# The gates of a two-layer token mixer computed between the steps of its branches and kept in DRAM until the merges

## The chip, the cores and the metric

The kernel runs on one core of a Trainium2 chip, as a single launch. The metric is the device time of that launch in microseconds (us). Before the change the median of three runs is 2623.72 us (2621.29 to 2623.99).

## The reference, cut to what matters

The network has two layers over 512 tokens of width 1024 (256 context tokens and 256 latent tokens). Each layer has a token mixer and a channel mixer, everything in float32. Only the token mixer is touched:

```python
def token_mixer(p, grid_rows, hy_p, cf_p, s5_p, s5_out_p, w_o, init, want_final):
    y_hy = hyena_branch(p[..., :CF_OFF], *hy_p)
    y_cf = conformer_branch(p[..., CF_OFF:S5_OFF], grid_rows, *cf_p)
    y_s5, finals = s5_branch(p[..., S5_OFF:GATE_OFF], s5_p, *s5_out_p, init, want_final)
    g_hy, g_cf, g_s5 = jnp.split(jax.nn.sigmoid(p[..., GATE_OFF:]), N_BRANCH, axis=-1)
    return (g_hy * y_hy + g_cf * y_cf + g_s5 * y_s5) @ w_o, finals
```

Here `p` is one projection of the modulated input, 6144 columns wide: 1536 for the long convolution (hyena), 1024 for the conformer branch (a gated unit and a depthwise convolution of 31 taps), 512 for the state-space branch (S5), and 3 x 1024 for the gates. A gate depends on the mixer's input alone. The second layer's mixer needs only the latent tokens, so it works on 256 of the 512; only the state-space branch there reads all of them.

## The kernel before, in words

**Products.** A float32 product is made of three matmuls: each operand is split into a high and a low part, and `mm3` (L128 to L133) adds high x high, low x high and high x low. A weight chunk of 512 KB (`wchunk`, L135 on) is loaded into a buffer `land`; of each half ScalarE writes the high part `wh` (L123) and VectorE the low part `wl` (L124). There are 4 `land` and 3 `wh`/`wl` buffers, and loads of chunks get a higher priority than what stands around them.

**One gate.** A gate is a tile of 128 channels by the layer's tokens. `gate` computes it from one chunk: `in_tile` issues 24 matmuls (8 slices of the contraction x 3) into a PSUM tile `p`, and ScalarE takes a tanh of it into a tile `mth`. A gate so costs one load, 2 casts on ScalarE, 2 subtractions on VectorE, 24 matmuls and one tanh. A layer has 24 gates, 8 for each branch.

**The mixer.** `mixer` issues, in this order: the projection for S5; the tiles of the long convolution (`hy_in`, short convolutions on VectorE); `s5_main`, four blocks, each of which runs through two groups of small matmuls (`ep`, `yp`) with a chain of VectorE and ScalarE work between them (L399 to L416); `hy_first` and `hy_second`, the two orders of the long convolution, as matmuls with DFT tables (`zc`, `zs` forward, `iv` inverse; in layer 0 for two sequences, in layer 1 for one); `conf_in`, whose result is `ub`; `s5_glu` (`gl`); and three merges, in the order S5, hyena, conformer. Before the last merge stands `conf_conv`, the 31 taps on VectorE (`dc`, L669). Last comes `proj_res`, the output projection (`acc`).

**A merge.** For each of four pairs of output tiles it computes two gates, loads one chunk of the branch's output weights, issues 2 x 12 matmuls (`bo`) and gates the result on VectorE: `mm = (mth + 1) * bo` in the first merge (L858), `mth = (mth + 1) * bo; mm += mth` in the others (L860, L861).

**Modulation work in layer 0.** During the merges of layer 0 a list `bg` of generators is advanced three steps per pair: the modulation vectors for the rest of the layer, whose weights `mw` are multiplied on VectorE (`ma`, L785 and L787; one of them on TensorE, `md`).

**What sets the order.** The program is written in the order above. A scheduler then orders each engine's instructions by priority (program order, chunks earlier) on a modelled timeline, so that matmuls of different steps interleave. On the chip each engine takes its instructions strictly in that order; all DMAs are issued by SyncE (SP), in one order too, and an SP instruction that waits for a buffer or for data holds up the loads behind it.

Of the kernel before, what the change touches and what calls it, by code (L numbers as in the profile page):

```python
# [10 lines left out]
FT = mybir.dt.float32  # L11
# [79 lines left out]
class Net:  # L91
# [264 lines left out]
    def s5_main(self, l, full):  # L356
        nc, sm = self.nc, self.sm
# [10 lines left out]
        f = lambda a: a.rearrange("p g j -> p (g j)")  # L368
        for b in range(NB):
            gs = slice(b * GB, (b + 1) * GB)  # L370
            U = U2[b // 2][:, (b % 2) * GB:(b % 2 + 1) * GB]
            we, wc = [], []
            for r in range(2):
                we.append(self.t4([128, GB, 128], "we", "XL"))
                nc.sync.dma_start(we[r].rearrange("p g m -> p (g m)"), sc["we"][b, r])
            tb = self.t4([128, 2, GB, 64], "tb", "XL")
            nc.sync.dma_start(tb.rearrange("p r g j -> p (r g j)"), sc["tb"][b])
            cs, sn = tb[:, 0], tb[:, 1]
            E = [128, GB, 64]
            ec = self.t4([128, 2, GB, 64], "ec", "XC")  # L380
            for r in range(2):
                ep = self.ps("ep", "aux")
                for g in range(GB):
                    nc.tensor.matmul(ep[:, g * 64:(g + 1) * 64], we[r][:, g], U[:, g], start=True, stop=True)
                nc.scalar.copy(ec[0:64, r].rearrange("p g j -> p (g j)"), ep[0:64])
                nc.scalar.copy(ec[64:128, r].rearrange("p g (s j) -> p g s j", s=2),
                               ep[64:128].rearrange("p (g s j) -> p g s j", g=GB, s=2)[:, :, :, ::-1])
            for r in range(2):
                wc.append(self.t4([128, GB, 128], "wc", "XL"))
                nc.sync.dma_start(wc[r].rearrange("p g m -> p (g m)"), sc["wc"][b, r])  # L390
            mt = self.t4([128, GB, 128], "mt", "U")
            nc.sync.dma_start(mt.rearrange("p g m -> p (g m)"), sc["m"][b])
            md = self.mx.tile(E, FT, name="md", tag="md5", bufs=1)
            nc.scalar.copy(md, mg[:, gs, None].to_broadcast(E))
            nc.gpsimd.memset(md[:, :, 0:1], 0.0)
            rr = self.t4([128, 2, GB, 64], "rr", "XC")
            for r in range(2):
                t1 = self.u2(E, "t1")
                nc.vector.tensor_tensor(rr[:, r], ec[:, r], cs, op=OP.mult)  # L399
                nc.vector.tensor_tensor(t1, ec[:, 1 - r], sn, op=OP.mult)  # L400
                nc.vector.tensor_tensor(rr[:, r], rr[:, r], t1, op=OP.add if r == 0 else OP.subtract)
            z = rr
            for r in range(2):
                nc.vector.tensor_tensor_scan(f(z[:, r]), f(md), f(rr[:, r]), 0.0, op0=OP.mult, op1=OP.add)
            sp = self.t4([128, 2, GB, 64], "sp", "XC")
            q = lambda a: a.rearrange("p g (s j) -> p g s j", s=2)
            for r in range(2):
                t1 = self.u2(E, "t1")
                t2 = self.u2(E, "t2")
                for t in (t1, t2):  # L410
                    nc.gpsimd.memset(t[:, :, 0:1], 0.0)
                nc.vector.tensor_tensor(t1[:, :, 1:], z[:, r, :, :63], cs[:, :, :63], op=OP.mult)
                nc.vector.tensor_tensor(t2[:, :, 1:], z[:, 1 - r, :, :63], sn[:, :, :63], op=OP.mult)
                nc.vector.tensor_tensor(t1, t1, t2, op=OP.subtract if r == 0 else OP.add)
                nc.scalar.copy(sp[0:64, r], t1[0:64])
                nc.scalar.copy(q(sp[64:128, r])[:, :, :, ::-1], q(t1[64:128]))  # L416
            yp = self.ps("yp", "aux")
            for g in range(GB):
                o = yp[:, g * nj:(g + 1) * nj]
                nc.tensor.matmul(o, mt[:, g], U[:, g, j0:], start=True, stop=False)  # L420
                nc.tensor.matmul(o, wc[0][:, g], sp[:, 0, g, j0:], start=False, stop=False)
                nc.tensor.matmul(o, wc[1][:, g], sp[:, 1, g, j0:], start=False, stop=True)
            a = self.u2([128, 512], "ya")
            w = self.u2([128, 512], "yq")
            e = slice(0, GB * nj)
            nc.scalar.activation(w[:, e], yp[:, e], AF.Square)
            nc.vector.scalar_tensor_tensor(w[:, e], w[:, e], 1.0 / 0.044715, yp[:, e], op0=OP.add, op1=OP.mult)
            nc.scalar.activation(w[:, e], w[:, e], AF.Tanh, scale=math.sqrt(2.0 / math.pi) * 0.044715)
            nc.vector.scalar_tensor_tensor(a[:, e], w[:, e], 1.0, yp[:, e], op0=OP.add, op1=OP.mult)
            v = lambda t: t[:, e].rearrange("p (g j) -> p g j", g=GB)  # L430
            for t in range(8):
                nc.sync.dma_start(sc["y"][gs, :, t, j0:].rearrange("g c j -> c g j"), v(a)[t * 16:(t + 1) * 16])

    def s5_glu(self, l, t0):
        nc, sm = self.nc, self.sm
# [172 lines left out]
        return k  # L608

    def hy_first(self, l, v, x0, seqs):  # L610
        k = self.hy_kk(l, 0)
        z1 = {}
        for s in seqs:
            vT = [self.t4([128, 2, 512], f"vT{a}", "Z", FR) for a in range(2)]
            self.hy_turn(v, s, vT)
            x0T = self.t4([128, 2, 512], "x0T", "Z")
            self.hy_turn(x0, s, [x0T])
            z1[s] = [self.t4([128, 2, 512], f"z1{a}", "Z", FR) for a in range(2)]

            def sink(tt, o, s=s, x0T=x0T):  # L620
                t = self.t2([128, 512], "zt")
                self.nc.vector.tensor_mul(t, o, x0T[:, tt])
                self.split(z1[s][0][:, tt], z1[s][1][:, tt], t)
            self.hy_conv(k, vT, 0, sink)
        return z1

    def hy_second(self, l, z1, x1, seqs):

        k = self.hy_kk(l, 1)
        for s in seqs:  # L630
            def sink(c, o, s=s):
                ss = slice(s * 256, (s + 1) * 256)
                self.nc.vector.tensor_mul(x1[c][:, ss], o, x1[c][:, ss])
            self.hy_conv(k, z1[s], 1, sink)
        return x1


# [193 lines left out]
    def gate(self, l, t0, j):  # L831
# [3 lines left out]
        nc.scalar.activation(th[:, t0:], self.in_tile(l, 24 + j, t0)[:, t0:], AF.Tanh, scale=0.5)  # L835
        return th

    def merge(self, l, t0, first, br, src, scale, mm):

        nc = self.nc  # L840
        bH = self.quad("bH", "K", FR)
        bL = self.quad("bL", "XC", FR)
        for j in range(4):
            self.split(bH[j][:, t0:], bL[j][:, t0:], src[j][:, t0:], scale=scale)
        for kp in range(4):
            if first:
                mm.append(self.t4([128, 2, 512], "mm", "Y"))
            ths = []
            for jj in range(2):
                ths.append(self.gate(l, t0, br * 8 + 2 * kp + jj))  # L850
            w = self.wchunk(self.i["w_bo"][l, br, kp], 8)
            for jj, th in enumerate(ths):
                o = self.ps("bo")
                for k in range(4):
                    self.mm3(o[:, t0:], w[jj * 4 + k], (bH[k][:, t0:], bL[k][:, t0:]), k == 0, k == 3)
                d = mm[kp][:, jj, t0:]
                if first:
                    nc.vector.scalar_tensor_tensor(d, th[:, t0:], 1.0, o[:, t0:], op0=OP.add, op1=OP.mult)  # L858
                else:
                    nc.vector.scalar_tensor_tensor(th[:, t0:], th[:, t0:], 1.0, o[:, t0:], op0=OP.add, op1=OP.mult)  # L860
                    nc.vector.tensor_add(d, d, th[:, t0:])  # L861
            self.pump(self.rate)
# [504 lines left out]
    def mixer(self, l, xin):  # L1367

        nc = self.nc
        full = l == 0  # L1370
        nts = (0, 1, 2, 3) if full else (2, 3)
        ws = (0, 1) if full else (1,)
        t0 = 0 if full else 256
        self.hsw = self.sm.tile([128, 12, 4], FT, name="hsw", tag="hsw", bufs=1)
        nc.sync.dma_start(self.hsw, self.i["hysw"][l])
        self.s5_in(l)
        self.pump(1000)
        v = self.hy_in(l, t0, 2)
        x0 = self.hy_in(l, t0, 0)
        self.s5_main(l, full)  # L1380
# [1 line left out]
        x1 = self.hy_in(l, t0, 1)  # L1382
        ho = self.hy_second(l, z1, x1, ws)
        cf = self.conf_in(l, t0)
        mm = []
        so = self.s5_glu(l, t0)
        self.rate = 0
# [14 lines left out]
    def body(self, dbg=None):  # L1402
        nc, tc = self.nc, self.tc
# [15 lines left out]
        c = self.const  # L1419
        self.mo, self.bg, self.rate = {}, [], 0  # L1420
        self.parts = 0
        self.s5sc = [self.s5_scratch(l) for l in range(2)]
        self.kd = [self.dram.tile([2, 2, 128, 2, 512], FT, name=f"kd{l}") for l in range(2)]
        xs = self.dram.tile([128, 4, 1024], FT, name="xs")
# [148 lines left out]
```

## Time and profile before

| | |
|---|---|
| median of three runs | 2623.72 us |
| the profiled execution, its own time | 2638.14 us |
| its span in the trace | 2636.3 us |
| TensorE (PE) busy | 2435.7 us, 92% |
| VectorE (DVE) busy | 2162.4 us, 82% |
| ScalarE (ACT) busy | 1373.0 us, 52% |
| mean granted TensorE clock | 0.941 |

The mixer of layer 0 runs from about 80 to 700 us, that of layer 1 from about 1222 to 1545 us. From 1560 us on the experts of layer 1 run, to the end.

Two marks cut each mixer where the change acts. The *branch stretch* runs from where the last tile of the long convolution's projections is through to the first `ub` (181 to 361.5 us in layer 0, 1276 to 1370.5 us in layer 1): S5 blocks and long convolutions. The *merge stretch* runs from the first `ub` to the first `acc` (361.5 to about 664 us, and 1370.5 to 1522 us): the conformer branch, `gl` and the three merges. A busy share is read against such a stretch, not against the whole span. The start-to-start distance of two matmuls is the time that one takes in a queue of them; the duration that a row gives for one is longer, since they overlap.

### The profile page before, as it was taken

The page shows a single profiled execution, that of the slowest core. Times are in us where ns is not written, and L with a number is a line of the kernel's source. Part 1 is how long each engine was busy: PE and PEld are TensorE (multiplying, and loading weights), DVE is VectorE, ACT ScalarE, POOL GpSimd, SP SyncE. Part 2 cuts the span into 40 slices and gives each one's busy share as a digit, 9 for nine tenths or more (in the row PEclk, how much of TensorE's full clock was granted, in tenths as well). Part 3 has the DMA queues.
Part 4 walks back from the last instruction along what each step waited for, and adds up shares of the span by engine and source line. Part 5 has one row for each costly group of instructions (what it writes and reads, how often), then busy time and mean ns, then how long its engine had stood idle before and what let it go on. Part 6 is the DMA issues. An engine that isn't in the chain of part 4 may idle for free. (4 is left out here: it accounts for less than half of the span.)

```text
span 2636.3 us, 34684 instructions
## 1 busy us (share of the span) xinstructions
PE 2435.7 (92%) x12312; PEld 2029.3 (77%) x12312; DVE 2162.4 (82%) x3182; ACT 1373.0 (52%) x1951; POOL 191.5 (7%) x202
## 2 busy tenths in 40 slices
PE   7888999999899998996999969999999999999986
PEld 2765886788787777885898958888887788878775
DVE  7886789994758988756789778888988789888997
ACT  3343442323453232323444527777877677777864
POOL 1620010000100022211000010000000000000000
PEclk8998899999999999997889979999999999999998
DMA  7455425542325554553545529998999898999984
GB/s 261 156 193 132 160 81 176 176 159 90 108 93 169 184 176 156 197 200 134 188 139 155 179 73 374 354 350 341 351 344 347 329 338 340 351 351 357 359 321 201
DMA packets 147349, 602.52 MB, mean 229 GB/s; under 512 B 41878, under 2 KB 42584, under 8 KB 104160
## 3 DMA queue, kind: packets, MB, share of 16 engines
q1 hardware_dynamic: 147168, 600.24, 63.9%
q8 instruction: 98, 1.61, 0.2%
q14 instruction: 83, 0.68, 0.1%
HBM read 563.96 MB, written 36.21 MB: 228 GB/s over the span
## 5 line engine op out<-in xcount | busy, mean ns | idle before, releaser
L124 DVE TENSOR_TENSOR mwl<-mland,mwh 128x1024 fp32r<-128x1024 f32 x672 | 788.6, 1220 | 79.1 <-ACT mwh L123 65.6
L123 ACT CAST mwh<-mland 128x1024 fp32r<-128x1024 f32 x672 | 675.2, 1052 | 122.6 <-PE mp L133 37.0
L123 ACT CAST wh<-land 128x512 fp32r<-128x512 f32 x396 | 244.6, 621 | 527.7 <-PE p L132 241.4
L124 DVE TENSOR_TENSOR wl<-land,wh 128x512 fp32r<-128x512 f32 x396 | 285.3, 723 | 119.4 <-ACT wh L123 109.2
L131 PE MATMUL p<-hh,wh 128*128 128x256 f32 (+1 forms) x800 | 277.9, 348 | 14.2 <-DVE q L549 8.9
L133 PE MATMUL p<-hh,wl 128*128 128x256 f32 (+1 forms) x800 | 278.2, 350 | 7.0 <-DVE wl L124 6.5
L132 PE MATMUL p<-hl,wh 128*128 128x256 f32 (+1 forms) x800 | 275.5, 345 | 0.1
L1154 PE MATMUL mp<-mwl,xg 128*128 128x512 f32 x560 | 223.9, 402 | 5.2 <-DVE mwl L124 5.1
L1154 PE MATMUL mp<-mwh,xg 128*128 128x512 f32 x560 | 221.2, 397 | 3.5 <-ACT mwh L123 2.8
L787 DVE SCALAR_TENSOR_TENSOR ma<-mw,sv,ma 128x512 f32<-128x512 f32 x196 | 153.5, 806 | 37.1 <-DMA mw<-in_w_mod 36.8
L131 PEld LDWEIGHTS p<-hh,wh 128*128 128x128 f32 x800 | 157.1, 197 | 34.2 <-issue 9.2
L131 PE MATMUL mp<-mwh,xg 128*128 128x512 f32 x448 | 178.0, 397 | 2.6 <-ACT mwh L123 2.6
L132 PE MATMUL mp<-mwl,xg 128*128 128x512 f32 x448 | 177.7, 397 | 1.7 <-DVE mwl L124 1.6
L133 PEld LDWEIGHTS p<-hh,wl 128*128 128x128 f32 x800 | 156.7, 196 | 28.8 <-DVE wl L124 12.0
L133 PE MATMUL mp<-mwh,xg 128*128 128x512 f32 x448 | 176.4, 394 | 0.0
L132 PEld LDWEIGHTS p<-hl,wh 128*128 128x128 f32 x800 | 157.1, 196 | 15.9 <-DVE hl L751 0.3
L133 PE MATMUL fo<-hh,wl 128*128 128x512 f32 (+1 forms) x384 | 147.4, 385 | 1.7 <-DVE wl L124 1.7
L131 PE MATMUL fo<-hh,wh 128*128 128x512 f32 (+1 forms) x384 | 147.6, 385 | 1.3 <-ACT hh L747 0.5
L132 PE MATMUL fo<-hl,wh 128*128 128x512 f32 (+1 forms) x384 | 146.1, 381 | 0.1
L669 DVE SCALAR_TENSOR_TENSOR dc<-ub,cfp,dc 128x512 f32<-128x512 f32 (+1 forms) x240 | 142.9, 622 | 0.6
L1154 PEld LDWEIGHTS mp<-mwl,xg 128*128 128x128 f32 x560 | 106.5, 190 | 30.9 <-DVE mwl L124 10.3
L1154 PEld LDWEIGHTS mp<-mwh,xg 128*128 128x128 f32 x560 | 106.5, 190 | 24.7 <-ACT mwh L123 4.6
(460 smaller groups left out, 4926.9 us busy)
## 6 DMA issues: line engine op xcount, KB each, us to landing
mland<-in_moe_w SPq DMA_DIRECT2D x336, 1024.0 KB, 6.9
mw<-in_w_mod SPq DMA_DIRECT2D x96, 512.0 KB, 3.5
land<-in_w_in SPq DMA_DIRECT2D x96, 512.0 KB, 3.6
land<-in_ffn_w SPq DMA_DIRECT2D x66, 512.0 KB, 4.0
land<-in_w_bo SPq DMA_DIRECT2D x24, 512.0 KB, 3.5
s5we<-weT SPq DMA_DIRECT2D x16, 512.0 KB, 4.0
s5wc<-sw SPq DMA_DIRECT2D x16, 512.0 KB, 2.9
we<-s5we SPq DMA_DIRECT2D x16, 512.0 KB, 5.7
```

The source lines that it names most:

```text
L123: nc.scalar.copy(h, src)
L124: nc.vector.tensor_sub(lo, src, h.bitcast(FT))
L131: nc.tensor.matmul(o, a[0], b[0], start=start, stop=False)
L132: nc.tensor.matmul(o, a[0], b[1], start=False, stop=False)
L133: nc.tensor.matmul(o, a[1], b[0], start=False, stop=stop)
L669: nc.vector.scalar_tensor_tensor(d, ub[:, :R, i:i + 64], cfp[:, j, i:i + 1], d, op0=OP.mult, op1=OP.add)
L787: nc.vector.scalar_tensor_tensor(ac[:, t], wk, self.sv[:, k, t:t + 1], ac[:, t], op0=OP.mult, op1=OP.add)
L1154: self.nc.tensor.matmul(o, x[0][:, i], w[r], start=start and r == 0, stop=stop and r == 1)
```

## The change

A generator `gates` makes the 24 gates of a layer in the order in which the merges use them and writes each to a DRAM tile (`gd`, 256 KB, of which layer 1 uses half). `fill(n)` advances it by n gates. It is called in `s5_main` after each of four blocks (2 gates), in `hy_first` and `hy_second` after each sequence (in layer 0: 1 and 2 gates for each of two sequences; in layer 1: 3 and 3 for its one), which are 14 gates in each layer, and once after `conf_in` for the remaining 10. `merge` no longer computes gates; it loads each from DRAM into an `mth` tile. The kind and number of matmuls, casts and vector instructions stay as they are; 48 writes and 48 loads of gates are added. In `mixer` the call `self.pump(1000)` (which empties `bg`) becomes a loop that pumps and fills while `bg` is not empty.

```diff
@@ s5_main, at the end of each of the four blocks
                 nc.sync.dma_start(sc["y"][gs, :, t, j0:].rearrange("g c j -> c g j"), v(a)[t * 16:(t + 1) * 16])
+            self.fill(2)
@@ hy_first, hy_second, at the end of each sequence
+        full = l == 0
...
             self.hy_conv(k, vT, 0, sink)
+            self.fill(1 if full else 3)
...
             self.hy_conv(k, z1[s], 1, sink)
+            self.fill(2 if full else 3)
@@ new
+    def gates(self, l, t0):
+
+        for br in (2, 0, 1):
+            for j in range(8 * br, 8 * br + 8):
+                th = self.gate(l, t0, j)
+                self.nc.sync.dma_start(self.gd[l][j][:, t0:], th[:, t0:])
+                yield
+
+    def fill(self, n):
+
+        for _ in range(n):
+            next(self.gq, None)
@@ merge
             for jj in range(2):
-                ths.append(self.gate(l, t0, br * 8 + 2 * kp + jj))
+                ths.append(self.t2([128, 512], "mth"))
+                nc.sync.dma_start(ths[-1][:, t0:], self.gd[l][br * 8 + 2 * kp + jj][:, t0:])
@@ mixer
+        self.gq = self.gates(l, t0)
         self.s5_in(l)
-        self.pump(1000)
+        while self.bg:
+            self.pump(4)
+            self.fill(1)
...
         cf = self.conf_in(l, t0)
+        self.fill(24)
@@ body
+        self.gd = [[self.dram.tile([128, 512], FT, name=f"gd{l}_{j}") for j in range(24)] for l in range(2)]
```

The scheduler places the gates further forward than they are written. The first place is on TensorE in layer 0, behind the last projection tile of the long convolution. Before, the transposes (`tq`) of the first convolution follow that tile (`p_1598`) at once:

```order
L133 MATMUL p_1598<-hh_99,wl_1606 128x512
L559 MATMUL tq_2090<-ident_110,q2_1328 128x128 [waits DVE_49,Activation_49]
L559 MATMUL tq_2090<-ident_110,q2_1328 128x128
L559 MATMUL tq_2090<-ident_110,q2_1329 128x128 x2
L493 MATMUL hp_976<-hid_963,w12_951 64x256 [waits DMAHW1_49,PE_49,Activation_49]
L559 MATMUL tq_2097<-ident_110,q2_1328 128x128 [waits DVE_49,PE_49]
```

Now the same place holds gates; these rows are the end of the second (`p_1850`) and the start of the third (`p_1995`), between matmuls of the long convolution's filters (`h3`):

```order
L131 MATMUL p_1850<-hh_147,wh_1857 128x512
L132 MATMUL p_1850<-hl_148,wh_1857 128x512
L133 MATMUL p_1850<-hh_147,wl_1858 128x512
L515 MATMUL h3_1044<-w3_1034,hid_1011 128x512 [waits Activation_49]
L515 MATMUL h3_1049<-w3_1034,hid_1011 128x512 [waits DVE_49]
L131 MATMUL p_1995<-hh_147,wh_1998 128x512 [waits Activation_49]
L132 MATMUL p_1995<-hl_148,wh_1998 128x512
```

Eight gates of layer 0 stand ahead of the first `tq`, six more among the convolutions and S5 blocks behind it. All `yp` and `iv` of the branches now stand ahead of the conformer's projection tiles, where the last of them used to interleave with these.

The second place is SP in the S5 blocks of layer 0, where loads of the blocks' tables (`wc`, `mt`, `we`, `tb`), of filters (`kk`) and of weights (`land`) are issued. Before:

```order
L432 DMA s5y0_87<-ya_1749 16x8x64 x8
L141 DMA land_2886<-in_w_in 128x1024
L390 DMA wc_1899<-s5wc0_82 128x1024
L390 DMA wc_1901<-s5wc0_82 128x1024
L375 DMA we_1977<-s5we0_81 128x1024
```

Now, between a block's result and the next block's table:

```order
L432 DMA s5y0_135<-ya_1797 16x8x64 x8
L848 DMA gd0_1_82<-mth_2728 128x512
L390 DMA wc_2099<-s5wc0_130 128x1024
L390 DMA wc_2101<-s5wc0_130 128x1024
L141 DMA land_3234<-in_w_in 128x1024
L141 DMA land_3272<-in_w_in 128x1024
```

The write of a gate (`gd0_1`) waits for that gate's tanh, and the `wc` loads stand behind it.

The third place is VectorE in the merge stretch of layer 0. Before, the S5 branch's last product (`so`) follows the start of the fourth convolution tile directly:

```order
L654 SCALAR_TENSOR_TENSOR ub<-cth,p 128x8x64
L124 TENSOR_TENSOR wl<-land,wh 128x512
L669 SCALAR_TENSOR_TENSOR dc<-ub,cfp,dc 128x512 x3
L124 TENSOR_TENSOR wl<-land,wh 128x512
L667 TENSOR_SCALAR dc<-ub,cfp 128x512
L461 SCALAR_TENSOR_TENSOR so<-gth,g_3042 128x8x64
```

Now the convolution's taps and the weight splits of the ten gates come between the two, 41 rows in all, of which these are the last:

```order
L674 SCALAR_TENSOR_TENSOR dc<-ub,cfp,dc 128x512 x3
L124 TENSOR_TENSOR wl<-land,wh 128x512
L674 SCALAR_TENSOR_TENSOR dc<-ub,cfp,dc 128x512
L462 SCALAR_TENSOR_TENSOR so<-gth,g_4002 128x8x64
L674 SCALAR_TENSOR_TENSOR dc<-ub,cfp,dc 128x512 x2
```

The taps move ahead of `so`, and all of `ma` now stands behind it, among the `bo` of the merges.

## Rows read from the trace of the kernel before

**Rows 1.** The profile page: span, and busy time of each engine.
```profile
span 2636.3 us, 34684 instructions
...
PE 2435.7 (92%) x12312; PEld 2029.3 (77%) x12312; DVE 2162.4 (82%) x3182; ACT 1373.0 (52%) x1951; POOL 191.5 (7%) x202
```
**Rows 2.** Busy time of each engine by stretch (instructions in brackets), with granted clock.
```profile
core 0: us, PE busy (x) PEld busy (x) DVE busy (x) ACT busy (x) POOL busy (x), PEclk, DMA share, GB/s
181.00:361.50 180.50, 157.72 (x769) 129.30 (x768) 126.37 (x205) 69.61 (x116) 3.50 (x21) 0.87 0.45 130
181.00:262.00 81.00, 63.30 (x228) 44.84 (x227) 50.37 (x85) 29.24 (x52) 0.22 (x2) 0.81 0.51 132
361.50:664.00 302.50, 295.00 (x1318) 232.29 (x1318) 253.80 (x407) 98.34 (x163) 13.39 (x11) 0.97 0.43 143
590.00:664.00 74.00, 72.81 (x334) 62.06 (x335) 33.35 (x57) 26.98 (x46) 0.18 (x1) 0.89 0.27 87
1276.00:1370.50 94.50, 88.96 (x547) 84.28 (x546) 77.88 (x130) 43.71 (x77) 3.29 (x19) 0.80 0.47 148
1370.50:1522.00 151.50, 145.97 (x1151) 141.91 (x1150) 131.97 (x290) 75.30 (x150) 2.09 (x3) 0.98 0.51 164
1482.00:1522.00 40.00, 38.69 (x326) 38.53 (x325) 25.95 (x55) 23.34 (x48) 0.70 (x1) 1.00 0.55 181
```
**Rows 3.** VectorE by line and form, 361.5 to 664 us: busy, mean ns, idle before.
```profile
L669 DVE SCALAR_TENSOR_TENSOR dc<-ub,cfp,dc 128x512 f32<-128x512 f32 x120 | 85.9, 743 | 0.2
L124 DVE TENSOR_TENSOR wl<-land,wh 128x512 fp32r<-128x512 f32 x89 | 61.0, 685 | 28.4 <-ACT wh L123 22.0 <-PE p L133 6.3
L787 DVE SCALAR_TENSOR_TENSOR ma<-mw,sv,ma 128x512 f32<-128x512 f32 x84 | 59.3, 741 | 0.0
```
**Rows 4.** VectorE by line and form, 590 to 664 us.
```profile
L124 DVE TENSOR_TENSOR wl<-land,wh 128x512 fp32r<-128x512 f32 x20 | 13.8, 690 | 24.0 <-ACT wh L123 17.7 <-PE p L133 6.3
```
**Rows 5.** TensorE by line and form, 590 to 664 us: the first of a gate's three matmuls.
```profile
L131 PE MATMUL p<-hh,wh 128*128 128x512 f32 x48 | 19.6, 409 | 0.0
```
**Rows 6.** Timeline of TensorE, layer 0: start, duration; nine starts apart in each pair.
```profile
256.48 0.63 PE L131 MATMUL p<-hh,wh 128*128 128x512 f32 x1
...
260.32 0.62 PE L131 MATMUL p<-hh,wh 128*128 128x512 f32 x1
...
261.25 0.39 PE L131 MATMUL p<-hh,wh 128*128 128x512 f32 x1
...
263.29 0.39 PE L131 MATMUL p<-hh,wh 128*128 128x512 f32 x1
```
**Rows 7.** Timeline of TensorE, layer 1: six starts apart.
```profile
1408.51 0.28 PE L131 MATMUL p<-hh,wh 128*128 128x256 f32 x1
...
1409.23 0.28 PE L131 MATMUL p<-hh,wh 128*128 128x256 f32 x1
```
**Rows 8.** Timeline of VectorE: a weight split and the instruction behind it.
```profile
409.80 0.67 DVE L124 TENSOR_TENSOR wl<-land,wh 128x512 fp32r<-128x512 f32 x1
410.40 0.73 DVE L669 SCALAR_TENSOR_TENSOR dc<-ub,cfp,dc 128x512 f32<-128x512 f32 x1
```
**Rows 9.** Timeline, TensorE and ScalarE: the first S5 block of layer 0.
```profile
248.21 2.18 PE L384 MATMUL ep<-U,we 128*128 128x64 f32 x9 [5.00 <-DMA U<-s5u]
...
255.93 0.58 ACT L386 COPY ec<-ep 64x512 f32<-64x512 f32 x1
...
278.95 0.33 PE L421 MATMUL yp<-sp,wc 128*128 128x64 f32 x2
```
**Rows 10.** Waits of TensorE, 181 to 361.5 us: total, times, longest.
```profile
PE kh L131 <- ACT hh L123: 6.6, 4, 2.1
```
**Rows 11.** VectorE by line and form, 1370.5 to 1522 us.
```profile
L124 DVE TENSOR_TENSOR wl<-land,wh 128x512 fp32r<-128x512 f32 x89 | 62.3, 702 | 9.2 <-ACT wh L123 9.1
```
**Rows 12.** DMA issues, 181 to 664 us: KB each, median us to landing.
```profile
kd<-ko SPq DMA_DIRECT2D x8, 256.0 KB, 2.7
...
g<-s5y SPq DMA_DIRECT2D x4, 256.0 KB, 5.0
```

More of the change, by code (lines that the diff above doesn't have):

```diff
@@ L624, in hy_first @@
             self.hy_conv(k, vT, 0, sink)
+            self.fill(1 if full else 3)
         return z1
     def hy_second(self, l, z1, x1, seqs):
+        full = l == 0
         k = self.hy_kk(l, 1)
```

## The prediction

> **What bounds the kernel now.** I read the page's first part, then busy time by stretch. Over the span TensorE is busy 92% and VectorE 82% [rows 1], which would make TensorE the bound; the stretches say something else [rows 2]. In layer 0's branch stretch (181 to 361.5 us) TensorE is busy 157.72 of 180.5 us and VectorE only 126.37: TensorE waits for short chains, and its clock is 0.87 of full speed. In the merge stretch (302.5 us) TensorE is busy 295.00, but VectorE, with 253.80, is idle mostly in one piece: of its 48.7 us of idle time 40.65 lie in the last 74 us, from 590 on, where it waits for casts and gates [rows 4] while TensorE is busy 72.81. Ahead of 590 it is idle 8 of 228.5 us. So the merge stretch is bound first by VectorE (taps 85.9, weight splits 61.0, modulation 59.3 us [rows 3]) and then, in its tail, by TensorE.
>
> **What moves.** No matmul, cast or vector instruction is added or taken away. In each layer 14 of 24 gates go from the merge stretch to the branch stretch; ten stay, ahead of `gl` instead of among the `bo`. The loop that replaces the pump finds `bg` already empty, so it adds no gates and costs nothing.
>
> *A gate's price.* Nine matmuls take 2.04 us at full clock, 0.227 each, and 3.84 us, 0.427 each, at the lower level [rows 6]; in layer 1, with half the columns, six take 0.72, 0.120 each [rows 7]. Of 24 matmuls a gate is 5.45 us in layer 0 and 2.88 in layer 1. On VectorE a gate is two splits of 0.60 us [rows 8], 1.2 us.
>
> *Layer 0, branch stretch: +56.* It gains 14 x 5.45 = 76.3 us of matmuls. What can hide them is its 22.8 us of idle and what the lower clock costs, 157.72 x 0.13 = 20.5 us, 43 us in all [rows 2]. If all of it fills, the first `ub` is 33 us later; if nothing does, 76. I take 20: eight gates stand directly in the first 81 us, where TensorE is idle 17.7 us (for filter parts `hh` 6.6, for the S5 input 5.0 [rows 9, 10]) at a clock of 0.81. Behind them little fills, since the S5 blocks form a chain, 22.4 us from the copy of `ec` (ended 256.51) to the `yp` that needs the scan (278.95) [rows 9], four times, and eight gates now stand ahead of its start: 76 - 20 = +56.
>
> *Layer 0, merge stretch: -60.* VectorE loses 28 splits (16.8 us) and about 6 us of the last S5 block, which now lies ahead of the first `ub` (an estimate: some ten instructions of 0.6 us), so 231 us of work are left. With the 8 us of idle that it has ahead of 590 that is 239, or -63.5. This needs the tail to vanish as a TensorE stretch. If the tail shrinks only by its own six gates (3 x 48 of its matmuls [rows 5], 32.7 us) and the part ahead of it only by VectorE's saving there (16 splits and the S5 block, 15.6), it is -48. I take -60, nearer to the row on VectorE, since the ten gates now run beside the taps, and modulation work can stand beside the last `bo`. Layer 0 gives -4.
>
> *Layer 1.* The branch stretch gains 14 x 2.88 = 40.3 us; its room is 5.5 us of idle and 88.96 x 0.20 = 17.8 of clock [rows 2]. Ends +17 and +40; with half of it filled, as in layer 0, +29. In the merge stretch VectorE has 131.97 us, less 16.8 for 28 splits and about 2.5 for the S5 block, and 5.5 of idle ahead of its own tail (19.53, less 14.05 from 1482 on): 118 of 151.5 us, or -33. The splits take 62.3 us here too [rows 11]. If the tail loses only its six gates (17.3 us) and the rest its splits, -29. I take -33: layer 1 gives -4.
>
> *The trip through DRAM: 0.* Two writes and two loads per pair are added, 96 transfers. The nearest rows: a write of 256 KB lands 2.7 us after its issue, a load of 256 KB that has just been written 5.0 us [rows 12]. A gate is loaded into an `mth` buffer and used behind 12 `bo` matmuls (2.7 us), and four such buffers let the next pair be loaded ahead; so I take 0. If every pair waited for a landing it is 12 x 5.0 = 60 us in layer 0. A write waits for its tanh at the head of SP's queue; behind it stand the `wc` loads of the S5 chain and the `land` loads of the next gates, so a late gate makes S5 late, which the ends above hold. Below nothing it can't be.
>
> *Sum.* -4 - 4 = -8 us on the profiled execution's 2638.1 us (span 2636.3), so 2630. That execution is 14.4 us above the median of 2623.7; on the median's scale the forecast is 2616. What I call no change is within 0.2%, 5.2 us, about what a measurement of this kernel can tell.
>
> **Rivals.**
>
> A. *The room fills almost whole.* The gates fill TensorE's waits and so also hold its clock up. For it: the waits are many and short [rows 10], a gate depends on nothing but the mixer's input and its weights, and the clock is lowest where gates now stand (0.81 and 0.80). Against it: each engine's order is fixed, so a gate that comes too early delays what is behind it. With all of the room layer 0 has +33 - 63 and layer 1 +17 - 33, -46 in all: 2578; with three quarters of it some 2596.
>
> B. *The gates stand in front of the chain* (the other side). On TensorE eight gates, 43.6 us, stand ahead of the first transposes and of S5's first `ep`; the chain of four blocks behind them runs no faster for it, and the waits of that chain stay. Then nothing of the room fills: +76 and +40. With the small gains of the merges, -48 and -29, that is +39, 2663; with the full ones, -60 and -33, it is +23, 2647. It decides from the point where less than 13 us of the 43 fill in layer 0: the delay then passes the 63.5 us that the merges can give back. For it: `ep` waits for data that comes back from DRAM [rows 9], and the loads of gate weights stand in SP's queue ahead of these. Against it: in the first 81 us 17.7 us of idle lie open.
>
> C. *The clock falls in the merges.* With VectorE as the bound of the merge stretch TensorE waits between `bo` groups. In layer 0 six conformer tiles, ten gates and `gl` (48 matmuls) take 98 us of the 239 that VectorE needs, and 288 `bo` (65.4 us at full clock) lie in the other 140 or so. In the branch stretches, where TensorE waits now, the granted clock is 0.87 and 0.80, in the merge stretches 0.97 and 0.98 [rows 2]. At the lower level the 288 `bo` take 288 x 0.427 = 123 us, 58 more. Most of that lies beside VectorE's 140; what sticks out is the end of each merge, some 10 to 25 us in the two layers: 2626 to 2641, or 2633. The Trainium skill (TensorE: Matmul & The Clock Gate, section A second HAM failure mode: psum-queue depth-cycling) says that frequent short idle times between groups of matmuls make the clock swing between its two levels, at a loss of throughput. By that rule this would be the case to expect; the trace agrees in so far as the stretches with waits have the low clock, and has no stretch in which `bo` groups wait for VectorE throughout.
>
> D. *Gates come back late.* The loads stand in SP's one order behind `land` loads that wait for buffers. For it: the 5.0 us [rows 12]; against it: four buffers. A third of the 60 us: 2636.
>
> **How the numbers follow.** The forecast's own case (a part of the room filled, VectorE the bound of the merges) has 0.46, with 2600 to 2632 (its delay in layer 0 from +43 to +70, layer 1 in step). A has 0.20, B 0.20, C 0.07, D 0.07. The range that leaves no more than 2 in 10 out goes from 2582, in the lower part of A, to 2652, in the lower part of B. Faster by over 0.2% means under 2618.5: A, somewhat over half of the forecast's case (0.28) and 0.02 of C and D where they come out mild, 0.50. Within 0.2% (to 2629): 0.12 of the forecast's case and 0.07 of the others, 0.19. Slower: the rest of it, B and most of C and D, 0.31.
>
> **What would show it.** The first `ub` at about 418 us instead of 361.5 (right from 405 to 428; A 395, B 438) and in layer 1 the branch stretch 29 us longer than its 94.5; the first `acc` 60 us sooner behind `ub` than the 302 it takes now, with VectorE busy at least 95% of that stretch; no idle of VectorE for `wl` in its tail (24.0 us now [rows 4]); the `mth` loads landed before their `bo`. I am wrong if the first `ub` comes later than 430, if TensorE's clock in the merges is below 0.85, or if VectorE waits for loaded gates for more than 5 us.

## The result, and the profile after

The changed kernel takes 2636.26 us (median of 11 runs) against 2622.02 us of the kernel before (11 runs): ratio 1.0054, 95% interval 1.0037 to 1.0071, or +14 us (+10 to +19). The forecast was 2616, 8 us faster. The sign is wrong. The time lies in the range, but that range reached up to the rivals B, C and D, so this says little for the forecast.

The two profiled executions don't show this. That of the kernel before took 2638.1 us, 16 us above its median, that of the changed kernel 2633.7, 3 us below its own. So I read stretches, not totals, and compare with a second profile of the kernel before (e1 below), of 2620.0 us. First the page of the changed kernel, its span and the busy time of each engine, to hold against [rows 1]:

```profile
span 2631.9 us, 34940 instructions
...
PE 2422.9 (92%) x12312; PEld 2022.2 (77%) x12312; DVE 2159.8 (82%) x3182; ACT 1372.1 (52%) x1951; POOL 185.7 (7%) x202
```

The instruction counts of the engines are the same, as the diff says. Then the changed kernel by stretch, with the columns of [rows 2]; 1261 us here is 1276 us there, since layer 1's mixer starts 15 us sooner than in that profile:

```profile
181.00:416.40 235.40, 224.24 (x1145) 189.38 (x1145) 152.78 (x241) 98.66 (x166) 4.98 (x23) 0.96 0.49 150
181.00:262.00 81.00, 79.88 (x345) 62.13 (x345) 47.49 (x78) 36.53 (x64) 0.23 (x2) 1.00 0.57 171
416.40:649.60 233.20, 214.69 (x942) 165.93 (x942) 225.20 (x367) 67.12 (x112) 6.57 (x9) 0.94 0.56 188
575.00:649.60 74.60, 62.04 (x312) 53.47 (x313) 73.62 (x128) 21.32 (x35) 1.45 (x1) 0.84 0.59 195
1261.00:1395.80 134.80, 128.72 (x921) 122.56 (x920) 98.59 (x162) 65.45 (x123) 4.66 (x21) 0.91 0.57 177
1395.80:1517.50 121.70, 106.25 (x771) 100.30 (x770) 107.66 (x249) 51.09 (x102) 0.70 (x1) 0.92 0.54 170
1441.00:1517.50 76.50, 61.05 (x398) 55.45 (x398) 62.91 (x152) 28.36 (x59) 0.70 (x1) 0.87 0.49 154
```

In layer 0 the first 81 us, where eight gates now stand, went from 17.7 us of idle TensorE and a clock of 0.81 [rows 2] to 1.1 us and 1.00. The branch stretch is 235.4 us long, the merge stretch 233.2, with VectorE busy 97% of it: the end of the merges is now VectorE's (73.62 of the last 74.6 us) and TensorE waits there, at a clock of 0.84. In layer 1 the branch stretch went from 94.5 to 134.8 us and the merge stretch from 151.5 to 121.7; behind 1441 us neither engine is the bound (TensorE 61.05, VectorE 62.91 of 76.5 us). VectorE's lines in layer 0's merge stretch, to hold against [rows 3]:

```profile
L674 DVE SCALAR_TENSOR_TENSOR dc<-ub,cfp,dc 128x512 f32<-128x512 f32 x120 | 83.8, 741 | 0.2
L792 DVE SCALAR_TENSOR_TENSOR ma<-mw,sv,ma 128x512 f32<-128x512 f32 x84 | 58.9, 741 | 2.4 <-DMA mw<-in_w_mod 2.4
L124 DVE TENSOR_TENSOR wl<-land,wh 128x512 fp32r<-128x512 f32 x60 | 40.9, 682 | 1.7 <-ACT wh L123 1.5
```

29 splits are gone (89 to 60), and the idle time ahead of them fell from 28.4 to 1.7 us. In the last 75 us of the merges, to hold against [rows 4]:

```profile
L124 DVE TENSOR_TENSOR wl<-land,wh 128x512 fp32r<-128x512 f32 x15 | 10.2, 679 | 0.0
```

VectorE no longer waits for splits there (24.0 us before). The loads of the gates hold nobody up: in layer 1 VectorE waited for one, once (total, times, longest):

```profile
DVE mth L879 <- PE bo L133: 3.8, 1, 3.8
DVE mth L879 <- DMA mth<-gd: 1.1, 1, 1.1
```

### The profile page after: what moved, and what is told of

It is laid out like the page before. It is cut to its first block, busy times and chain, and to the rows that moved or that the text cites. A ratio compares the mean times of both kernels' runs of the same rounds, so it can differ in the third digit from the quotient of the medians.

```text
span 2631.9 us, 34940 instructions
## 1 busy us (share of the span) xinstructions
PE 2422.9 (92%) x12312; PEld 2022.2 (77%) x12312; DVE 2159.8 (82%) x3182; ACT 1372.1 (52%) x1951; POOL 185.7 (7%) x202
## 5 line engine op out<-in xcount | busy, mean ns | idle before, releaser
L132 PE MATMUL mp<-mwl,xg 128*128 128x512 f32 x448 | 178.9, 399 | 1.5 <-DVE mwl L124 1.5
L674 DVE SCALAR_TENSOR_TENSOR dc<-ub,cfp,dc 128x512 f32<-128x512 f32 (+1 forms) x240 | 137.0, 610 | 0.3
```

The source lines that it names most:

```text
L132: nc.tensor.matmul(o, a[0], b[1], start=False, stop=False)
L674: nc.vector.scalar_tensor_tensor(d, ub[:, :R, i:i + 64], cfp[:, j, i:i + 1], d, op0=OP.mult, op1=OP.add)
```

## The experiments

Each kernel was timed in turn with the kernel before. "L0" and "L1" are the mixers of the two layers, each as branch stretch + merge stretch (L0 from 181 us, L1 from its first `ep`; both to the first `acc`). Over all profiles with an unchanged mixer L0 takes 465 to 482 us (mean of eight 473, of which 176 branch), L1 269 to 274 (mean of nine 270.5, of which 118 branch). The mark between the two stretches is the first `ub`; what the scheduler puts ahead of it differs between kernels, so the sum of both says more than either.

| | what is changed | ratio (95%) | L0, us | L1, us |
|---|---|---|---|---|
| e8 | the change again | 1.0052 (1.0037 to 1.0067) | 238.3 + 236.2 | 165.4 + 121.4 |
| e2 | layer 0 alone | 0.9990 (0.9974 to 1.0007) | 237.3 + 237.7 | 119.6 + 152.3 |
| e3 | layer 1 alone | 1.0033 (1.0017 to 1.0049) | 175.3 + 294.1 | 160.6 + 119.5 |
| e4 | all 24 in one block | 1.0112 (1.0092 to 1.0132) | 174.6 + 320.2 | 115.7 + 152.6 |
| e5 | L0: 8 early, 16 in merges | 0.9955 (0.9940 to 0.9971) | 195.8 + 260.4 | 115.8 + 153.5 |
| e6 | L1: 6 early, 18 in merges | 1.0068 (1.0051 to 1.0086) | 173.4 + 301.6 | 147.6 + 128.2 |
| e7 | loads of gates left out | 1.0073 (1.0055 to 1.0091) | 233.9 + 242.2 | 161.6 + 121.0 |
| e9 | a tiny instruction alone | 0.9992 (0.9978 to 1.0007) | 178.9 + 294.2 | 119.1 + 151.0 |
| e10 | e6, experts' order kept | 1.0036 (1.0023 to 1.0050) | 176.4 + 302.0 | 149.5 + 127.3 |
| e11 | e3, experts' order kept | 1.0045 (1.0030 to 1.0059) | 174.5 + 294.8 | 161.0 + 118.9 |
| e12 | e5, experts' order kept | 0.9951 (0.9933 to 0.9969) | 197.3 + 260.6 | 115.8 + 153.3 |
| e13 | L0: 14 early, 10 in merges | 1.0032 (1.0016 to 1.0048) | 235.8 + 245.3 | 120.4 + 150.7 |
| e14 | L0: 8 early, 16 in a block | 1.0012 (0.9998 to 1.0025) | 200.4 + 274.6 | 121.4 + 152.6 |
| e15 | L0: 12 early with S5, 12 in merges | 1.0024 (1.0010 to 1.0038) | 235.5 + 242.7 | 118.2 + 150.8 |
| e16 | L1: 14 early, 10 in merges | 1.0055 (1.0035 to 1.0076) | 176.4 + 295.0 | 164.6 + 119.4 |

**Which layer pays (e1 to e3).** The edit of e2 and e3 makes merges of the other layer compute their gates as before:

```diff
-        self.gq = self.gates(l, t0)
+        self.gq = self.gates(l, t0) if l == 0 else iter(())   # e2; l == 1 in e3
```

> The kernel before, unchanged: a second profiled execution of it. The one shown took 2638 us, 16 us above the median of its runs (2622), that of the changed kernel 2634, 2 us below its median (2636), so the two profiles can't be subtracted. Theory 1 (layer 1 pays, layer 0 is near zero): the 16 us lie in layer 0's mixer, whose first acc then comes at about 646 to 650 us here instead of 662.6, with a total near 2622. Rival (the 16 us lie elsewhere, in the feed-forward part or the experts): the first acc comes at 660 or later again and a later stretch is shorter.

> The change in layer 0 alone; in layer 1 the gates stay in the merges. Theory 1 (TensorE in layer 1's branch stretch was already busy 112.4 of 118 us, so nothing fills there; layer 0 comes out near even): +0 to +6 us. Rival 1 (the trip through DRAM on SyncE's queue costs about the same per gate in both layers): +7. Rival 2 (layer 0's moves carry the loss): +12 to +16.

> The change in layer 1 alone; in layer 0 the gates stay in the merges. Theory 1: +8 to +12 us, with the branch stretch 40 us longer and the merge stretch 30 us shorter than before. Rival 1 (the trip through DRAM): +7. Rival 2 (layer 0 carries the loss): 0 to +2.

Theory 1 held in the main: layer 0 alone is -3 us (-7 to +2), layer 1 alone +9 (+4 to +13). Together that is +6, where the change gave +14, and +14 again in e8. Before e8 I had put +5 to +9 if the layers add up and +12 or more if something works only with both; e11 below gives +12 for layer 1 and so +9 for both. The few us that are left stay open. The second profile of the kernel before has its first `acc` at 646.2 us. By stretch (branch and merge of layer 0, then of layer 1):

```profile
181.00:352.00 171.00, 149.72 (x769) 121.94 (x768) 125.99 (x204) 69.62 (x116) 3.50 (x21) 0.91 0.43 137
352.00:646.20 294.20, 287.25 (x1311) 226.07 (x1311) 252.39 (x405) 97.42 (x162) 13.42 (x11) 0.99 0.44 146
1236.90:1354.70 117.80, 112.36 (x743) 107.68 (x744) 93.40 (x158) 56.70 (x99) 3.40 (x20) 0.84 0.52 169
1354.70:1506.60 151.90, 146.96 (x1153) 143.35 (x1153) 132.30 (x290) 75.36 (x151) 2.09 (x3) 0.97 0.52 164
```

and layer 1 with the change, in e3:

```profile
1241.80:1402.40 160.60, 154.77 (x1116) 148.51 (x1117) 113.89 (x190) 79.01 (x145) 4.80 (x22) 0.90 0.59 185
1402.40:1521.80 119.40, 105.29 (x770) 100.11 (x769) 108.47 (x250) 51.11 (x103) 0.70 (x1) 0.90 0.56 175
```

Add TensorE's busy time over both stretches: 259.3 us before, 260.1 with the change. It is the same work at the same price; TensorE's idle time is what differs, 10.4 us before (5.4 of it in the branch stretch) and 19.9 after (14.1 of it in the merges). Layer 1's mixer was TensorE's through and through: there were 10.4 us of waits to gain, and the change added 9.5.

The branch stretch also took over the end of the last S5 block. Its `yp` used to stand partly behind the first `ub` and now all stand ahead of it. Here are the two stretches of layer 1 in e1 for `yp` alone (in e3 none of it is left in the merges), and, last, those of layer 0's merges in e1:

```profile
1236.90:1354.70 117.80, 25.09 (x148) 25.02 (x148) 2.52 (x6) 1.15 (x3) 0.84 0.52 169
1354.70:1506.60 151.90, 6.64 (x44) 6.63 (x44) 0.85 (x2) 0.42 (x1) 0.97 0.52 164
352.00:646.20 294.20, 5.24 (x46) 5.29 (x46) 1.34 (x2) 0.65 (x1) 0.99 0.44 146
```

**One block, and no loads (e4, e7).**

> All 24 gates of each layer in one block behind the conformer's projection, none between the steps; the trip through DRAM stays. Theory 1: the branch stretches are as long as before; the block is bound by TensorE (layer 0: 24 gates 131 us, six conformer tiles and gl 44, beside some 115 us of VectorE work) and the rest by VectorE (about 134 us in layer 0), so layer 0's merge stretch is about 309 us instead of 302 and layer 1's about 165 instead of 152: +20 in all, more than the changed kernel. Rival 1 (the trip through DRAM is the loss): the same as the changed kernel, +14. Rival 2 (gates between the steps of layer 0 are the loss): faster than the changed kernel, 0 to +7.

> The changed kernel, but the merges read a fixed tile in place of the gates, so the 48 loads of gates are left out (their writes stay). Theory 1 (the loads are hidden; layer 1's merge waits for VectorE's chains): merge stretches as in the changed kernel within 3 us each (233 and 122), +9 to +14 us against before. Rival (loads that wait for buffers at the head of SyncE's queue hold up the weights behind them): layer 0's merge stretch 225, layer 1's 112, so -4 to +2.

e4 drops the calls of `fill` between the steps. It came out at +29 us, beyond theory 1's +20, and both rivals are out: L0 lost 22 us, though L1 nothing where 13 were expected. The rest lies behind the mixers, as in e6 (see the order of the experts). e7 reads a fixed tile in the merges:

```diff
-                nc.sync.dma_start(ths[-1][:, t0:], self.gd[l][br * 8 + 2 * kp + jj][:, t0:])
+                g = self.dfs[0][:, 0].bitcast(FT)[:, t0:]   # in place of the gate, in both products
```

Layer 1's merges took 121.0 us without the loads and 121.4 and 121.7 with them, and the whole was no faster (+0.7%, above the 9 to 14 us that were expected). The trip's loads cost nothing that shows; what the writes cost wasn't tried alone.

**Fewer gates (e5, e6).** `fill(2)` stays in `s5_main` in e5 (layer 0) and `fill(3)` in the two orders of the long convolution in e6 (layer 1); gates that are not made early are computed in the merges:

```diff
+                j = br * 8 + 2 * kp + jj
+                if j in self.early:      # e5: 8 to 15 in layer 0; e6: 10 to 15 in layer 1
...
+                else:
+                    ths.append(self.gate(l, t0, j))
```

> In layer 0 only the eight gates of the last merge (conformer) are made early, two after each S5 block; the other sixteen, and all of layer 1, stay in the merges. Theory 1 (a gate moved gives back its TensorE time while the merge stretch is bound by TensorE, and the branch stretch of layer 0 has room for some 12 to 20 us): 8 gates are 43.6 us; branch stretch +24 to +32, merge stretch -38 to -44, together -6 to -16 us. Rival (gates ahead of the S5 chain find no room): +0 to +5.

> In layer 1 only six gates of the last merge are made early (three after each order of the long convolution), eighteen stay; layer 0 as before the change. Theory 1 (nothing fills in layer 1's branch stretch, but its merge stretch gives back a gate's whole time while it is bound by TensorE, and less only beyond some eight gates): branch +17 to +19, merge -16 to -18, together 0 to +2 us. Rival (each moved gate costs its share, by the trip or by the order): 6/14 of 9, +4.

e5 is faster than both kernels: 2612.21 us against 2624.33, -12 us (-16 to -8). Its branch and merge stretch in layer 0:

```profile
181.00:376.80 195.80, 185.18 (x967) 154.03 (x967) 142.00 (x228) 87.59 (x145) 3.60 (x21) 0.97 0.50 157
376.80:637.20 260.40, 249.95 (x1120) 194.79 (x1119) 238.74 (x386) 81.48 (x134) 7.67 (x11) 0.96 0.46 151
```

Eight gates (43.6 us) make the branch stretch 20 us longer than the mean of the unchanged ones and the merge stretch 37 us shorter. Over both, TensorE is idle 21 us (28.2 in e1) and busy 435.1 us; in the eight unchanged profiles it is idle 28 to 30 us and busy 437 to 451. So some 7 us of the gain are waits filled; the rest is TensorE's busy time, which also spreads from profile to profile. In the change six more gates make the branch stretch another 40 us longer for 25 us of merges. e6 is a miss: the six gates cost 5 us in L1 where 0 to 2 were expected, by waits for the S5 chain (in e10, the same mixer; in e1 this wait is 4.1 us, once):

```profile
PE yp L421 <- ACT sp L416: 9.1, 2, 5.0
```

So in layer 1 six moved gates already cost, as the rival had it.

**The order of the experts (e9 to e12).** e6 was 18 us slower, its mixer only 5. The scheduler orders by a modelled timeline, so a shift of a mixer re-orders the unchanged experts. Tiny instructions ahead of the routing shift that timeline too, with the mixers untouched. One was meant to give the experts e6's order, other counts of it to bring the old order back:

```diff
+            for i in range(1):    # e9; 3 in e10, 5 in e11, 4 in e12
+                nc.vector.tensor_scalar(xr[3][:, 0:64], xr[3][:, 0:64], 1.0, None, op0=OP.mult)
             rest = self.route(xr)
```

> The kernel before with one tiny VectorE instruction (128 x 64, a multiplication by one) ahead of the routing of layer 1. Both mixers are ordered as before; but the modelled timeline shifts, and the scheduler puts the experts' matmuls into exactly the order that they have in the kernel with six early gates in layer 1 (e6). Theory 3 (a moved instruction also re-orders the unchanged experts, and that order has a price of its own: e6 came out at +18 us, of which its mixer showed only 6): +6 to +12 us. Rival (the order of the experts is free, e6's surplus lay in its mixer): 0 to +2 us.

> Six early gates in layer 1 as in e6, with three tiny VectorE instructions ahead of the routing, with which the scheduler leaves the experts in the order of the kernel before, row for row. Theory 3: only the mixer's own +4 to +8 us are left of e6's +18. Rival: +15 to +20 again.

> All fourteen early gates in layer 1 alone (as e3), with five tiny VectorE instructions ahead of the routing, with which the experts stand in the order of the kernel before. Theory 1 (layer 1's mixer pays the gates' own time, 44 us longer in the branches, 31 us shorter in the merges): +10 to +14 us. Rival (e3's +9 is what the mixer costs): +7 to +9.

> The eight gates of layer 0's last merge early (as e5, -12 us), with four tiny VectorE instructions ahead of the routing, with which the experts stand in the order of the kernel before. Theory 1 (the gain is layer 0's mixer): -10 to -16 us. Rival (a lucky order of the experts gave a part): -2 to -8.

e10 to e12 have the old order: in their traces TensorE's rows behind the routing stand as in the kernel before, one by one. e9 does not have e6's order. The first place where these part is a group of matmuls early in the experts (kernel before, e9, e6):

```profile
1594.61 0.75 PEld L1123 LDWEIGHTS xgp<-oh,hmx 128*128 128x128 f32 x5
1586.06 0.75 PEld L1123 LDWEIGHTS xgp<-oh,hmx 128*128 128x128 f32 x5
1597.65 0.97 PEld L1145 LDWEIGHTS xgp<-oh,hmx 128*128 128x128 f32 x7
```

These are weight loads, which stand in the order of the matmuls; the line numbers differ because the files do. From there on e6's rows keep differing up to the end of the experts; e9 follows the kernel before up to its last 63 us, and has row by row the order of e3 and e16. So e9 (-2 us, -6 to +2) shows that one small re-ordering is free, and doesn't test theory 3. What tests it is e6 against e10: the same mixer, whose L1 takes 275.8 and 276.8 us, and the experts in another order, +18 us (13 to 23) against +9 (6 to 13). Theory 3 had +4 to +8 for e10, its rival +15 to +20, so e10 speaks for theory 3. Behind the mixer (e10, then e6, then e9):

```profile
1524.00:2638.50 1114.50, 1038.15 (x4944) 861.98 (x4942) 965.09 (x1133) 799.58 (x962) 10.84 (x12) 0.96 0.86 324
1523.30:2644.40 1121.10, 1045.04 (x4944) 867.44 (x4942) 965.30 (x1130) 799.02 (x961) 10.83 (x12) 0.95 0.86 322
1513.80:2622.50 1108.70, 1035.52 (x4934) 858.72 (x4932) 961.51 (x1122) 797.93 (x958) 10.83 (x12) 0.96 0.86 325
```

The eight profiles with the old order take 1110.6 to 1116.8 us there, e4, with yet another order, 1122.4. But e13, whose order is nearly the old one, takes 1121.0 in its one profile, so it is the whole times of e6 and e10 that carry this, and why e6's order is slower isn't shown. The change has an order of its own there too and takes 1114.4 to 1117.7 us (its profile, e7 and e8), e3 1107.9; this may be what the two layers lack of +14. With the experts' order held, layer 1's fourteen gates cost 12 us (8 to 15), six cost 9 (6 to 13), and e5's gain stands (-13, -18 to -8).

**Where the gain of the eight goes (e13 to e16).**

> Layer 0 only: fourteen gates early, at the same fourteen places as in the change (eight with S5, six with the convolutions), but the other ten stay in the merges among the bo instead of in one block. Theory 4 (the block does it: without gates among the bo, TensorE waits there for VectorE at a lower clock): merge stretch shorter than the changed kernel's plus its block, together -8 to -14 us. Rival (the six gates among the convolutions find no room): branch stretch +58 to +62, merge -58 to -62: -2 to +2 us.

> Layer 0 only: eight gates early as in e5, but the other sixteen in one block behind the conformer's projection instead of in the merges. Theory 4 (the block costs): branch +21 as in e5, merge only -18 to -24 instead of -37: 0 to +4 us. Rival (the six gates among the convolutions cost): -10 to -14 as e5.

> Layer 0 only: twelve gates early, three with each S5 block, none with the convolutions, twelve left in the merges. Theory (the room of layer 0's branch stretch, 23 us, is full after eight gates, and the merges give back a gate's whole time until VectorE bounds them, some 50 us): branch +42 to +48, merge -50 to -58: -6 to -12 us, no better than eight. Rival (room grows with every gate): -18 or more.

> Layer 1 only: fourteen gates early at the change's places, the other ten left in the merges among the bo. Theory 4 (the block costs): layer 1's merge stretch about 112 us instead of 121, with a clock above 0.95, and +2 to +5 us in all. Rival (layer 1 has no room, whatever is done in the merges): merge 118 to 122, +9 to +13 us.

Behind the mixers e14 and e15 have the experts in the old order, e16 in that of e9, e13 nearly in the old one. e14 came out as theory 4 had it (+3 us): with the same eight early gates, the block costs 14 us of merge stretch (274.6 against 260.4). Its parts, the block with `gl` and the rest:

```profile
381.40:507.30 125.90, 125.90 (x574) 104.01 (x573) 116.05 (x177) 39.06 (x66) 6.63 (x10) 1.00 0.40 124
507.30:656.00 148.70, 123.01 (x548) 91.57 (x546) 123.09 (x208) 42.17 (x69) 1.45 (x1) 0.89 0.67 222
```

In the block TensorE is busy throughout; behind it both engines wait a sixth of the time, where in e5 VectorE was busy 238.74 of 260.4 us over the whole merge. But theory 4 is no general rule: with fourteen early, leaving the ten in the merges is worse than the block (e13, +8 us, where -8 to -14 was expected; merges 245.3 against some 236). Why isn't shown. e15 is a miss too, +6 us instead of -6 to -12. Its branch stretch (the first 81 us, and the rest) shows why:

```profile
181.00:262.00 81.00, 81.00 (x342) 63.77 (x341) 39.56 (x65) 36.38 (x63) 0.23 (x2) 1.00 0.53 181
262.00:416.50 154.50, 141.39 (x761) 122.77 (x761) 111.41 (x175) 60.84 (x99) 4.70 (x21) 0.88 0.40 123
```

The first 81 us are full, and all twelve gates stand ahead of the first transposes (the first `tq` starts at 267.3 us); in the chain behind them TensorE is idle 13.1 us at a clock of 0.88, more than behind eight gates (e5: 8.7 us, 0.96); why it waits more isn't shown. So the branch stretch grew by 60 us where 42 to 48 were expected. The merges gave the 54 us that were expected, but each step gives less: 260.4 us with eight early gates, 242.7 with twelve, some 236 with fourteen, VectorE busy 92%, 95% and 95 to 97% of them. In layer 1 e16 shows the rival right: without a block the merge stretch is 119.4 us, no shorter, and the whole +14.

## Why the prediction was wrong, point by point

*What bounds the kernel.* Right for layer 0: VectorE bounds the merges once gates leave them (97% busy), and the tail's waits for splits are gone. Wrong for layer 1. There I read the merge stretch as VectorE's by its work left (118 us) and the branch stretch as having 23 us of room; but TensorE was busy 259.3 of 269.7 us in the two together, so it was the bound of both.

*Layer 0, branch +56, merge -60.* Measured 235.4, 238.3 and 237.3 us of branch (the change, e8, e2) against a mean of 176, +61; merges 233.2, 236.2 and 237.7 against 297, -61. The mechanism and the sizes held; layer 0 gives about nothing where -4 was forecast. The 5 us are a term left out: I moved the end of the last S5 block for VectorE, but not its 46 `yp` for TensorE (5.24 us in e1's merges). With these, 81.5 us came into the branch stretch, and 20 of them filled, as forecast. Room was found where I had put it, in the first 81 us. Over both stretches TensorE is idle as long as before, 29.7 us against 28.2 in e1: what the branch stretch filled opened again in the merges.

*Layer 1, branch: "with half of it filled, as in layer 0, +29". This is the step that failed.* Measured 158 to 165 us in four profiles against 118: +40 to +47, 43 in the mean. The forecast let 11 of 40.3 us vanish in 23 us of room. With the 44 `yp` (6.64 us), which it left out here too, 47 us came, so about 4 of the 23 filled. Of the idle time nothing filled: 5.4 us before, 5.8 in e3. The other 17.8 us were the lower clock taken as room. The clock did rise, from 0.84 over e1's whole stretch to 0.90 in e3, and TensorE's busy time grew by 42.4 us (112.36 to 154.77) for those 47 us of work. But the merges gave this back: 47 us of work left them, at a clock that fell from 0.97 to 0.90, and their busy time fell by 41.7 us only. Over both stretches the clock gained nothing (259.3 and 260.1 us).

*Layer 1, merge -33.* Measured 118.9 to 121.7 us against 152, -30 to -33: right in size. But of the 41.7 us of busy time that left (146.96 to 105.29) only 32.5 came off the stretch. The rest is idle time of TensorE beside a VectorE that is busy 91% of it in e3.

*The trip through DRAM, 0.* Held for the loads (e7). The loop over `bg` does nothing, by the code: the list is empty there.

*The sum.* Layer 0 about 0 and layer 1 +11 (281.7 us in the mean of four profiles against 270.5) make +11, against +14 (+10 to +19) measured; the forecast was -4 and -4. None of the three signs of being wrong came: the first `ub` of layer 0 at 416.4 us, the clock of the merges at 0.94 and 0.92, 1.1 us of waits for a loaded gate. None of them looked at layer 1's branch stretch.

*The rivals.* B came nearest, but for layer 1 alone, where it had +40 and -29 to -33; in layer 0 its point of decision was not passed. C is partly there: the clock in the merges fell from 0.99 to 0.94 in layer 0 and from 0.97 to 0.92 in layer 1, where TensorE is now idle 18.5 and 15.5 us instead of 6.9 and 4.9 (e1). The Trainium skill (TensorE: Matmul & The Clock Gate, A second HAM failure mode: psum-queue depth-cycling) says that frequent short idle times between groups of matmuls make the clock swing between its levels, at a loss of throughput; the trace agrees as to the clock of the merges. That it cost anything over the mixer isn't shown: TensorE's busy time in layer 0, which holds the slow matmuls too, is 437 to 451 us in the eight unchanged profiles, and 439, 446 and 445 in the change, e8 and e2. D, gates that come back late, is out by e7.

## What to carry to other kernels

Before work is moved from one stretch to another, add the busy and idle time of the engine that carries it over both: in layer 1 TensorE idled 10.4 of 269.7 us, so there was little to gain, however empty one stretch looked beside its clock. Where there is room, move as much as fills it, and leave the rest where it stands: here 8 of 24 gates in one layer gave -12 us, and 12, 14, or 8 with the others in a block gave nothing or lost. A lower clock in a stretch is not room by itself: in layer 1 the merges lost what the branch stretch got back. And move everything that crosses the mark for both engines, not for one.

## What the runs showed that I had not expected

One execution of the same program can differ by 16 us from the median of its kind, and it does so in the part under study (layer 0's mixer took 481.6 us in one profile of the kernel before and 465.2 in another), so two single profiles say nothing about a change of this size. The 16 us are not waits: TensorE was idle 30.3 and 28.2 us, and busy 451 and 437, at a clock of 0.87 and 0.97 in the two stretches of one and 0.91 and 0.99 in those of the other. And a change re-orders code behind it that it doesn't touch: e6 and e10 differ by three tiny instructions and by 9 us.
